# The z/u stage of a hybrid decoder layer: low parts one block later, sums and chain copies earlier, norms moved into v's stage, half of x first

## The chip, the cores and the metric

One core of a Trainium2 chip runs the whole program in one launch. The metric is the time of one execution on the device, in microseconds (us); the kernel before took 1266.7 us in the median of three runs (1266.69 to 1267.68). The engines in this text are PE (matmul), DVE (VectorE), ACT (ScalarE), POOL (GpSimd) and SP, which here only issues loads.

## The reference, cut to what matters

```python
h = x @ w_in[i]                         # x: 1024 tokens x 1024
u = gelu(h[..., 3*D_ATTN : 3*D_ATTN + D_GMLP])
z = gelu(h[..., 3*D_ATTN + D_GMLP :])
gm = _chunked_gmlp(u, z, ...)           # u * (W_s @ LN(z) + b)
mix = concat([attention(q, k, v), gm]) @ w_o
x = LN1(ALPHA * x + mix)                # then the convolved feed-forward, LN2,
x = LN3(ALPHA * x + gate * ple)         # and the gated input embedding
```

All data are float32. Only the first part, z, u and the v that follows, is touched by the change.

## The kernel before, in words

A float32 product is made of three matmuls with values that are split in a high and a low part (`mm3`, lines 131 to 134). `split` (line 115) makes them: ACT copies the source into a high part, DVE subtracts that from the source, which gives the low part. A matmul of 128x128 by 128x512 is the unit of work.

z and u are 1024 x 512 each, and h is made from x (both halves of its 1024 columns) by a Strassen scheme with seven products instead of eight. Tokens come in four pairs of 128 (`tp` or `j`), an "even" and an "odd" block in each pair. The even blocks with the first and the second half of x's columns are a11 and a12 of the scheme, the odd ones a21 and a22; the weights are the blocks "11", "21" (of z's columns) and "12", "22" (of u's), each in two pieces of 128 x 2 x 512. Product p takes four token blocks (`xop_of`) and one weight block (`wst[p, s]`, two pieces) and runs 48 matmuls: `zu_product` goes through the four k blocks of 128 columns and in each through the four j (product 0: j outside). Products 0, 3, 4 and 6 add into the PSUM chain X (`zbank`, the two tiles zA), product 1 into Y, products 2 and 5 into Z; Y and Z lie in the same four banks (B, B, D0, D1). `zu_evac` takes a chain's value out after a product: ACT copies it (p = 0, 2, 3; a Gelu for 6), DVE adds it to what lies in z or u (1, 4, 5). `s_sum` makes the sums S1 to S4 of x's blocks on DVE, in place where the raw x lies (S3 into half of a z page), `s_split` splits them, and `t_sum` makes the sums of the weights in place of the raw weights. The raw x of the first column half lies in the tile u.

The order is written by hand (`manual_schedule`): each engine runs its instructions in the order of the Python program, and waits by semaphores for the data and for buffers. Buffers come from pools: 12 weight pieces ("w"), 24 pages ("pg"), two raw buffers ("raw"), three large ones ("L"). SP issues loads in the program's order too, so a load that waits for a buffer holds back those behind it.

Then comes v (`dense_pair`, tile vps): it needs the even and odd blocks of x and the four pieces of a further weight (`Wv`). x's odd blocks of the first column half are loaded once more (256 KB each, into the raw buffers), since their place is u's by then. `z_norm` is a layer norm of one block of z and its split; two are done before v, six within it. v's first tiles are those of the chain X, so v waits for z's last copies (`zu_evac(6, j)`).

Of the kernel before, what the change touches and what calls it, by code (L numbers as in the profile page):

```python
# [51 lines left out]
def hybrid_layer(ctx, tc, x, xT, pT, pos, w_in, ln_z_g, ln_z_b, w_sT, b_sT, w_o,  # L52
# [134 lines left out]

    def put_x(kh, i, src):
        X[kh][i] = page([128, 2, 4, 128], F32R, "xhl")
        split(X[kh][i][:, 0], X[kh][i][:, 1], src)  # L190
# [59 lines left out]
    load_x(1, 3)  # L250
    SP.dma_start(ident, c_id)
# [15 lines left out]
    for k in range(1, 4):  # L267
        first_x(k)
# [64 lines left out]
    def s3raw(tp):  # L333
        return zp[tp][:, 1, :].rearrange("p (k c) -> p k c", c=128)

    def s_split(n, tp):
        if n > 2:
            d = sop[n + 1, tp] = page([128, 2, 4, 128], F32R, "zs")
            split(d[:, 0], d[:, 1], s3raw(tp) if n == 3 else raw_x(1, tp, 0))
# [4 lines left out]
        split(d[:, 0], d[:, 1], raw_x(0, tp, 2 - n))  # L344

    zu_product(0)
# [3 lines left out]
    split_wraw(1, "21", 1)  # L350
    zu_product(1)
    for s_ in range(2):
        load_wraw("12", s_)
    for s_ in range(2):
        load_wraw("22", s_)
# [5 lines left out]
    for s_ in range(2):  # L361
# [5 lines left out]
    zu_product(2)  # L367
    for tp in range(4):
        s_sum(2, tp)
        s_split(2, tp)  # L370
    def t_sum(dst, a, b, s_):
        DVE.tensor_tensor(wraw[dst, s_], wraw[a, s_], wraw[b, s_], OP.subtract)

    t_sum("11", "22", "11", 0)
    split_wraw(3, "11", 0)
    t_sum("11", "22", "11", 1)
    split_wraw(3, "11", 1)
    zu_product(3)
    for tp in range(4):
        s_sum(3, tp)  # L380
        s_split(3, tp)
    t_sum("12", "22", "12", 0)
    split_wraw(4, "12", 0)
    for tp in range(4):
        s_sum(4, tp)
    for j in range(4):
        zu_evac(3, j)
    t_sum("12", "22", "12", 1)
    split_wraw(4, "12", 1)
    for j in range(4):  # L390
        zu_evac(2, j)
        ACT.activation(zp[j][:, 0, :], zp[j][:, 0, :], AF.Gelu)
# [3 lines left out]
    split_wraw(5, "22", 0)  # L396
    split_wraw(5, "22", 1)
    for tp in range(4):
        put_x(1, 2 * tp + 1, raw_x(1, tp, 1))
    for s_ in range(2):  # L400
        t_sum("21", "21", "11", s_)
    for j in range(4):
        zu_evac(4, j)
    zu_product(5)
# [3 lines left out]
    for s_ in range(2):  # L408
        split_wraw(6, "21", s_)
    for j in range(4):  # L410
        ACT.activation(u[:, 2 * j + 1, :], u[:, 2 * j + 1, :], AF.Gelu)
    znh = big([128, NT, 512], F32R, "znh")
    znl = big([128, NT, 512], F32R, "znl")

    def z_norm(i):
        zz = zp[i // 2][:, i % 2, :]
        ln_dve(zz, zz, *ln_stats(zz, 512), gbz[:, 0, :], gbz[:, 1, :])
        split(znh[:, i, :], znl[:, i, :], zz)

    for j in range(4):  # L420
        zu_evac(5, j)
# [55 lines left out]
    for j in range(4):  # L477
        pa = psA("vps")
        g = dense_pair(j, W, pa)
        if j == 0:  # L480
            next(g)
            z_norm(1)
            next(g)
            z_norm(3)
        if j == 1:
            next(g)
            z_norm(4)
            next(g)
            z_norm(6)
        if j == 2:  # L490
            next(g)
            z_norm(5)
            next(g)
            z_norm(7)
# [768 lines left out]
    n = 0  # L1263
# [372 lines left out]
```

## Time and profile before

| | us |
|---|---|
| median of three runs | 1266.7 |
| profiled execution | 1266.69 |
| span of that execution (first to last instruction) | 1265.0 |
| PE busy | 1205.4 (95%) |
| DVE busy | 888.1 (70%) |
| ACT busy | 562.8 (44%) |
| first matmul of v | 121.75 |

The profiled execution lies 1.7 us above its span, at the fastest of the three runs. A timeline gives an instruction's start and length; in brackets stands the idle time of its engine before it, and what ended that. The length of a matmul is modelled and overlaps the next one's start, so its pace is read from one start to the next.

### The profile page before, as it was taken

To read this page: it belongs to the slowest core of one execution; us is meant where nothing else is said; L and a number is where in the kernel's file an instruction comes from. 1 tells how busy PE (TensorE), PEld (TensorE's weight loads), DVE (VectorE), ACT (ScalarE), POOL (GpSimd) and SP (SyncE) were. 2 spreads that over 40 slices of the span, in tenths; PEclk is the share of its full clock that TensorE was granted. 3 is DMA by queue.
4 is the path that set the end of the run, shared out by engine and by line. 5 is a ranking of instruction groups with operands and counts; after the bars stand their busy time and mean duration, and the time that the engine had idled before them with its cause. 6 is when DMAs were issued, how large, how long until landed. Compare 5 with 4: busy or idle time off the path is not lost. (4 is left out here: it accounts for less than half of the span.)

```text
span 1265.0 us, 15813 instructions
## 1 busy us (share of the span) xinstructions
PE 1205.4 (95%) x5788; PEld 1003.3 (79%) x5788; DVE 888.1 (70%) x1319; ACT 562.8 (44%) x972; POOL 467.9 (37%) x371
## 2 busy tenths in 40 slices
PE   8784999998999997999999999999999999999997
PEld 6673888887887886888888888888878888888886
DVE  4675653435788888576667776667776985798876
ACT  4263221437786672553443443444454344541221
POOL 0000100233342645666677766677710000022443
PEclk8897999999999999999999999999999999999999
DMA  7013254320020213203333213333379544640001
GB/s 285 0 34 104 80 200 167 117 67 18 1 84 34 84 59 127 67 2 124 125 125 125 87 47 117 125 125 125 96 263 340 194 128 130 217 164 26 34 34 50
DMA packets 64125, 136.93 MB, mean 108 GB/s; under 512 B 5552, under 2 KB 25392, under 8 KB 64048
## 3 DMA queue, kind: packets, MB, share of 16 engines
q1 hardware_dynamic: 62176, 129.51, 30.0%
q10 hardware_dynamic: 1872, 6.42, 1.3%
q8 instruction: 45, 0.74, 0.2%
q14 instruction: 32, 0.26, 0.1%
HBM read 101.05 MB, written 34.87 MB: 107 GB/s over the span
## 5 line engine op out<-in xcount | busy, mean ns | idle before, releaser
L166 POOL TENSOR_TENSOR rs<-rs,neg 128x1 f32<-128x1 f32 x24 | 21.1, 877 | 398.3 <-DVE rs L165 398.3
L132 PE MATMUL P<-xop,wop 128*128 128x512 f32 (+1 forms) x376 | 146.2, 389 | 0.0
L134 PE MATMUL P<-xop,wop 128*128 128x512 f32 (+1 forms) x376 | 145.3, 386 | 0.0
L133 PE MATMUL P<-xop,wop 128*128 128x512 f32 (+1 forms) x376 | 145.1, 386 | 0.0
L117 POOL TENSOR_TENSOR wop<-s,wop 128x512 fp32r<-128x512 f32 x62 | 94.2, 1525 | 86.4 <-ACT wop L111 86.4
L117 POOL TENSOR_TENSOR wop<-raw,wop 128x512 fp32r<-128x512 f32 x64 | 101.3, 1597 | 35.3 <-ACT wop L111 35.1
L111 ACT ACTIVATE aop<-raw 128x512 fp32r<-128x512 f32 x77 | 48.2, 626 | 92.1 <-DMA raw<-hid_d 65.2
L111 ACT ACTIVATE wop<-s 128x512 fp32r<-128x512 f32 x66 | 41.3, 626 | 99.8 <-DVE s L1163 53.4
L134 PEld LDWEIGHTS P<-xop,wop 128*128 128x128 f32 x376 | 71.2, 189 | 14.1
L132 PEld LDWEIGHTS P<-xop,wop 128*128 128x128 f32 x376 | 71.2, 189 | 13.9
L133 PEld LDWEIGHTS P<-xop,wop 128*128 128x128 f32 x376 | 71.2, 189 | 13.8
L117 DVE TENSOR_TENSOR aop<-raw,aop 128x512 fp32r<-128x512 f32 x77 | 56.8, 738 | 23.1 <-ACT aop L111 23.1
L1238 DVE SCALAR_TENSOR_TENSOR ht<-ct,mask,ht 128x1023 f32<-128x1023 f32 x22 | 47.9, 2176 | 31.4 <-ACT ht L1237 31.3
L133 PE MATMUL P<-bop,aop 128*128 128x512 f32 x176 | 68.8, 391 | 0.6 <-DVE bop L117 0.6
L132 PE MATMUL P<-bop,aop 128*128 128x512 f32 x176 | 68.6, 390 | 0.0
L134 PE MATMUL P<-bop,aop 128*128 128x512 f32 x176 | 68.5, 389 | 0.0
L111 ACT ACTIVATE wop<-raw 128x512 fp32r<-128x512 f32 x66 | 39.6, 626 | 61.6 <-DMA raw<-in_w_b_dram 39.0
L132 PE MATMUL D<-xop,wop 128*128 128x512 f32 (+1 forms) x176 | 66.9, 380 | 0.0
L134 PE MATMUL D<-xop,wop 128*128 128x512 f32 (+1 forms) x176 | 66.8, 379 | 0.0
L133 PE MATMUL D<-xop,wop 128*128 128x512 f32 (+1 forms) x176 | 66.8, 379 | 0.0
L1245 POOL TENSOR_TENSOR ht<-ht,ct 128x1024 f32<-128x1024 f32 x22 | 57.2, 2598 | 14.5 <-ACT ht L1242 14.5
L111 ACT ACTIVATE ct<-P 128x512 f32<-128x512 f32 x68 | 40.3, 593 | 45.4 <-PE P L134 42.8
(366 smaller groups left out, 3502.5 us busy)
## 6 DMA issues: line engine op xcount, KB each, us to landing
raw<-hid_d SPq DMA_DIRECT2D x35, 512.0 KB, 3.9
hid_d<-ct SPq DMA_DIRECT2D x22, 512.0 KB, 5.6
wd<-in_w_down_dram SPq DMA_DIRECT2D x44, 256.0 KB, 5.8
hid_d<-ht SPq DMA_DIRECT2D x33, 256.0 KB, 4.7
raw<-in_w_in_dram SPq DMA_DIRECT2D x12, 512.0 KB, 3.5
raw<-in_w_a_dram SPq DMA_DIRECT2D x11, 512.0 KB, 4.0
raw<-in_w_b_dram SPq DMA_DIRECT2D x11, 512.0 KB, 6.0
wraw<-in_w_a_dram SPq DMA_DIRECT2D x11, 512.0 KB, 5.5
```

The costliest lines, as they stand in the source:

```text
L111: ACT.activation(dst, src, AF.Copy)
L117: lo_eng.tensor_tensor(lo, src, hi.bitcast(F32), OP.subtract)
L132: PE.matmul(ps, sh, mh, start=first, stop=False, skip_group_check=chain)
L133: PE.matmul(ps, sh, ml, start=False, stop=False, skip_group_check=chain)
L134: PE.matmul(ps, sl, mh, start=False, stop=last, skip_group_check=chain)
L166: POOL.tensor_tensor(rs, rs, neghalf, OP.pow)
L1238: DVE.scalar_tensor_tensor(t[:, 1:S], c[:, 0:S - 1], cw[:, f, 1:2], t[:, 1:S], op0=OP.mult, op1=OP.add)
L1245: POOL.tensor_tensor(tt[g, e], tt[g, e], ctile[g, 1, e], OP.mult)
```

## The change

It has five parts.

- Low parts wait in a list (`lows`). `split_d` issues the high part on ACT at once and keeps DVE's subtraction back until the next block's high part has been issued; `flush` empties the list. Weight blocks are split, and their sums made, in halves of 128x512.
- `s_sum` runs one block ahead of its split; the S3 and S4 sums are made before the second weight piece of product 3, ahead of the splits that need a free page; the chain copies `evacs(p)` stand earlier, in front of the next weight sum, and the Gelu of z is no longer between chain 2's copies.
- Of the first column half of x, the even blocks are loaded first and the odd ones behind all of x's second half.
- SP's reloads for v alternate: two of x, two weights, two of x, two weights; the norm's vectors (`gbz`) come behind them, not ahead.
- The two z norms ahead of v move into v's first three pairs, and each norm's scaling stands behind the next one's statistics.

On DVE, from chain 1's adds to the sums for product 3 (L327 and L340 are S2's sums, L362, L372 and L361 weight sums, L117 and L196 low parts; zs and wil are the low parts' tiles, L342 and L344 the S3 and S4 sums). Before:

```order
L362 TENSOR_TENSOR wraw<-wraw 128x1024
L117 TENSOR_TENSOR wil<-wraw,wih 128x1024
L327 TENSOR_TENSOR u<-u 128x4x128
L117 TENSOR_TENSOR zs<-u,zs 128x512
L327 TENSOR_TENSOR u<-u 128x4x128
L117 TENSOR_TENSOR zs<-u,zs 128x512
L327 TENSOR_TENSOR u<-u 128x4x128
L117 TENSOR_TENSOR zs<-u,zs 128x512
L327 TENSOR_TENSOR u<-u 128x4x128
L117 TENSOR_TENSOR zs<-u,zs 128x512
L372 TENSOR_TENSOR wraw<-wraw 128x1024
L117 TENSOR_TENSOR wil<-wraw,wih 128x1024
```

Now:

```order
L196 TENSOR_TENSOR zs<-u,zs 128x512
L340 TENSOR_TENSOR u<-u 128x4x128
L196 TENSOR_TENSOR zs<-u,zs 128x512 x2
L361 TENSOR_TENSOR wraw<-wraw 128x512 x2
L196 TENSOR_TENSOR zs<-u,zs 128x512
L196 TENSOR_TENSOR wil<-wraw,wih 128x512 x2
L342 TENSOR_TENSOR z<-raw,u 128x512
L342 TENSOR_TENSOR z<-xraw,u 128x512 x3
L344 TENSOR_TENSOR raw<-raw,u 128x4x128
L344 TENSOR_TENSOR xraw<-xraw,u 128x4x128 x3
L361 TENSOR_TENSOR wraw<-wraw 128x512 x2
L196 TENSOR_TENSOR wil<-wraw,wih 128x512 x2
```

The low parts of S2 no longer alternate with its sums, a weight's sum and its low part have other work between them, and eight x sums stand ahead of the second weight piece.

On ACT, ahead of v (L429 and L457 are u's Gelu, L304 and L317 z's last copies, the wih are v's weights, znh the norms' high parts). Before:

```order
L111 ACTIVATE xhl<-raw 128x512 x4
L429 ACTIVATE u<-u 128x512 x4
L111 ACTIVATE wih<-raw 128x1024 x3
L111 ACTIVATE znh<-z 128x512 x2
L304 ACTIVATE z<-zA 128x512 x4
L111 ACTIVATE wih<-raw 128x1024
L111 ACTIVATE znh<-z 128x512 x2
```

Now:

```order
L111 ACTIVATE xhl<-raw 128x512 x2
L111 ACTIVATE wih<-raw 128x1024 x2
L111 ACTIVATE xhl<-raw 128x512 x2
L457 ACTIVATE u<-u 128x512 x4
L317 ACTIVATE z<-zA 128x512 x4
L111 ACTIVATE wih<-raw 128x1024 x2
L111 ACTIVATE znh<-z 128x512 x2
```

z's last copies now stand ahead of the third weight and of all norms, and behind the second pair of reloaded x.

On SP, from the last z/u weights to v (L425 and L445 are the reloads of x, gbz the norm's vectors). Before:

```order
L229 DMA wraw<-in_w_in_dram 128x1024 x4
L137 DMA gbz<-in_ln_z_g_dram 128x512
L137 DMA gbz<-in_ln_z_b_dram 128x512
L425 DMA raw<-in_xT_dram 128x4x128 x4
L125 DMA raw<-in_w_in_dram 128x1024 x4
L513 DMA raw<-in_w_sT_dram 128x1024
```

Now:

```order
L240 DMA wraw<-in_w_in_dram 128x1024 x4
L445 DMA raw<-in_xT_dram 128x4x128 x2
L125 DMA raw<-in_w_in_dram 128x1024 x2
L445 DMA raw<-in_xT_dram 128x4x128 x2
L125 DMA raw<-in_w_in_dram 128x1024 x2
L137 DMA gbz<-in_ln_z_g_dram 128x512
L137 DMA gbz<-in_ln_z_b_dram 128x512
L547 DMA raw<-in_w_sT_dram 128x1024
```

The norm's vectors moved behind v's loads, which alternate now.

The diff, cut to its core:

```diff
+    lows = []
+    def flush(keep=0):
+        while len(lows) > keep:
+            lows.pop(0)()
+    def split_d(hi, lo, src, keep=1):
+        copy(ACT, hi, src)
+        lows.append(lambda: DVE.tensor_tensor(lo, src, hi.bitcast(F32), OP.subtract))
+        flush(keep)
     def put_x(kh, i, src):
-        split(X[kh][i][:, 0], X[kh][i][:, 1], src)
+        split_d(X[kh][i][:, 0], X[kh][i][:, 1], src)
...
     def split_wraw(p, blk, s):
-        split(hi, lo, wraw[blk, s])
+        for k in range(2):
+            split_d(hi[:, k], lo[:, k], wraw[blk, s][:, k])
...
     SP.dma_start(r0[:, 0:1], w_in[4, 0][:, 0:1])
-    SP.dma_start(x0[:, 0:1], xT[0, 0, :, 0:1, :])
+    SP.dma_start(x0[:, 0:2, 0:128], xT[0, 0, :, 0:2, 0:128])
     SP.dma_start(r0[:, 1:2], w_in[4, 0][:, 1:2])
-    for k in range(1, 4):
-        SP.dma_start(x0[:, k:k + 1], xT[0, 0, :, k:k + 1, :])
+    SP.dma_start(x0[:, 2:4, 0:128], xT[0, 0, :, 2:4, 0:128])
     load_wraw("11", 1)
     for tp in range(1, 4):
-        load_x(0, tp)
+        stage_x(0, tp)
+        SP.dma_start(raw_x(0, tp, 0), xT[0, tp, :, :, 0:128])
...
     load_x(1, 3)
+    for tp in range(4):
+        SP.dma_start(raw_x(0, tp, 1), xT[0, tp, :, :, 128:256])
...
-    for j in range(4):
-        zu_evac(0, j)
+    evacs(0)
+    s_sum(1, 0)
     for tp in range(4):
-        s_sum(1, tp)
+        if tp < 3:
+            s_sum(1, tp + 1)
         s_split(1, tp)
-    for s_ in range(2):
-        DVE.tensor_tensor(wraw["11", s_], wraw["12", s_], wraw["11", s_], OP.subtract)
-        split_wraw(2, "11", s_)
-        if s_ == 0:
-            for j in range(4):
-                zu_evac(1, j)
+    t_sum("11", "12", "11", 0)
+    split_wraw(2, "11", 0)
+    flush()
+    evacs(1)
+    t_sum("11", "12", "11", 1)
+    split_wraw(2, "11", 1)
+    flush()
     zu_product(2)
...
     split_wraw(3, "11", 0)
+    flush()
+    for tp in range(4):
+        s_sum(3, tp)
+    for tp in range(4):
+        s_sum(4, tp)
     t_sum("11", "22", "11", 1)
     split_wraw(3, "11", 1)
+    flush()
     zu_product(3)
     for tp in range(4):
-        s_sum(3, tp)
         s_split(3, tp)
     t_sum("12", "22", "12", 0)
     split_wraw(4, "12", 0)
-    for tp in range(4):
-        s_sum(4, tp)
-    for j in range(4):
-        zu_evac(3, j)
+    flush()
+    evacs(3)
     t_sum("12", "22", "12", 1)
     split_wraw(4, "12", 1)
...
+    evacs(5)
+    zu_product(6)
+    def reload_x(tp):
+        r = rawpage([128, 4, 128])
+        SP.dma_start(r, xT[0, tp, :, :, 128:256])
+        put_x(0, 2 * tp + 1, r)
+    Wv = group(2)
+    reload_x(0)
+    reload_x(1)
+    flush()
+    Wv.load(2)
+    reload_x(2)
+    reload_x(3)
+    flush()
+    for j in range(4):
+        ACT.activation(u[:, 2 * j, :], u[:, 2 * j, :], AF.Gelu)
+    evacs(6)
+    Wv.load(2)
...
-    Wv.load(3)
-    z_norm(0)
-    z_norm(2)
-    for j in range(4):
-        zu_evac(6, j)
-    Wv.load(1)
...
+        if j < 3:
+            for i in ((0, 2, 1), (3, 4, 6), (5, 7))[j]:
+                next(g)
+                z_norm(i)
```

## Rows read from the trace of the kernel before

**Rows 1.** The page, part 1: busy time, share of the span, instructions.
```profile
span 1265.0 us, 15813 instructions
...
PE 1205.4 (95%) x5788; PEld 1003.3 (79%) x5788; DVE 888.1 (70%) x1319; ACT 562.8 (44%) x972; POOL 467.9 (37%) x371
```

**Rows 2.** Waits of PE, 0 to 240 us: total us, times, longest.
```profile
PE vps L132 <- ACT z L304: 16.4, 1, 16.4
PE zA L132 <- ACT wih L111: 7.5, 2, 4.4
PE zA L132 <- ACT u L111: 3.8, 1, 3.8
PE B L132 <- DVE z L308: 1.8, 1, 1.8
```

**Rows 3.** Timeline of PE: start us, length, line, operation, [idle before <- releaser].
```profile
11.11 0.80 PE L132 MATMUL zA<-wih,xhl 128*128 128x512 f32 x1 [3.10 <-ACT wih L111]
...
12.38 0.80 PE L133 MATMUL zA<-wil,xhl 128*128 128x512 f32 x1 [0.47 <-DVE wil L117]
...
17.60 0.40 PE L133 MATMUL zA<-wil,xhl 128*128 128x512 f32 x1
...
24.19 0.39 PE L132 MATMUL B<-wih,xhl 128*128 128x512 f32 x1
...
36.99 0.47 PE L132 MATMUL B<-wih,zs 128*128 128x512 f32 x1 [1.76 <-DVE z L308]
...
52.51 0.79 PE L132 MATMUL zA<-wih,zs 128*128 128x512 f32 x1 [4.36 <-ACT wih L111]
...
70.75 0.50 PE L132 MATMUL zA<-wih,zs 128*128 128x512 f32 x1 [3.85 <-ACT u L111]
...
121.75 0.79 PE L132 MATMUL vps<-wih,xhl 128*128 128x512 f32 x1 [16.44 <-ACT z L304]
```

**Rows 4.** Windows: length, busy PE, PEld, DVE, ACT, POOL; clock; DMA share, GB/s.
```profile
30.00:40.00 10.00, 8.24 (x37) 6.52 (x36) 7.87 (x10) 1.83 (x3) 0.00 (x0) 1.00 0.02 7
...
53.00:54.00 1.00, 0.53 (x2) 0.24 (x2) 1.00 (x2) 0.00 (x0) 0.00 (x0) 0.50 0.00 0
```

**Rows 5.** Timeline of DVE, 43 to 71 us, columns as in rows 3.
```profile
43.48 0.69 DVE L117 TENSOR_TENSOR zs<-u,zs 128x512 fp32r<-128x512 f32 x1 [0.70 <-ACT zs L111]
...
65.16 1.22 DVE L372 TENSOR_TENSOR wraw<-wraw 128x1024 f32<-128x1024 f32 x1
...
69.33 1.89 DVE L331 TENSOR_TENSOR xraw<-xraw,u 128x512 f32<-128x512 f32 x3
```

**Rows 6.** Timeline of ACT, 3 to 123 us, columns as in rows 3.
```profile
3.54 0.63 ACT L111 ACTIVATE wih<-wraw 128x512 fp32r<-128x512 f32 x1 [1.46 <-DMA wraw<-in_w_in_dram]
...
10.01 1.06 ACT L111 ACTIVATE wih<-wraw 128x1024 fp32r<-128x1024 f32 x1 [2.52 <-DMA wraw<-in_w_in_dram]
...
21.52 0.63 ACT L111 ACTIVATE xhl<-xraw 128x512 fp32r<-128x512 f32 x1 [0.62 <-DMA xraw<-in_xT_dram]
...
69.53 2.38 ACT L111 ACTIVATE u<-zA 128x512 f32<-128x512 f32 x4 [1.98 <-DVE raw L331]
...
101.14 2.18 ACT L429 ACTIVATE u<-u 128x512 f32<-128x512 f32 x4
...
120.64 2.04 ACT L304 ACTIVATE z<-zA 128x512 f32<-128x512 f32 x4
```

**Rows 7.** DMA per half us, 0 to 20; u's loads; L425, L125 landing.
```profile
GB/s 0 0 0 45 164 379 260 160 199 127 277 311 389 344 369 361 410 410 410 418 393 434 426 401 434 401 401 418 418 442 401 410 393 401 401 426 426 382 358 374
...
u<-in_xT_dram SPq DMA_DIRECT2D x3, 512.0 KB, 8.0
...
DMA to landing us min/median/max: 3.1/3.9/4.7
...
DMA to landing us min/median/max: 3.4/3.5/4.9
```

**Rows 8.** Windows of 25 us, columns as in rows 4.
```profile
600.00:625.00 25.00, 25.00 (x112) 20.70 (x111) 15.54 (x15) 12.41 (x21) 18.18 (x13) 1.00 0.45 158
```

More of the change, by code (lines that the diff above doesn't have):

```diff
@@ L266, in hybrid_layer @@
     first_w(1)
-    for k in range(1, 4):
-        first_x(k)
+    first_x(2)
     split_wraw(0, "11", 1)
@@ L338, in s_split @@
             d = sop[n + 1, tp] = page([128, 2, 4, 128], F32R, "zs")
-            split(d[:, 0], d[:, 1], s3raw(tp) if n == 3 else raw_x(1, tp, 0))
+            split_d(d[:, 0], d[:, 1], s3raw(tp) if n == 3 else raw_x(1, tp, 0))
             return
@@ L343, in s_split, with t_sum, evacs @@
         d = sop[n + 1][:, tp]
-        split(d[:, 0], d[:, 1], raw_x(0, tp, 2 - n))
+        split_d(d[:, 0], d[:, 1], raw_x(0, tp, 2 - n))
+    def t_sum(dst, a, b, s_):
+        for k in range(2):
+            DVE.tensor_tensor(wraw[dst, s_][:, k], wraw[a, s_][:, k], wraw[b, s_][:, k], OP.subtract)
+    def evacs(p):
+        for j in range(4):
+            zu_evac(p, j)
+    flush()
     zu_product(0)
@@ L350, in hybrid_layer @@
     split_wraw(1, "21", 1)
+    flush()
     zu_product(1)
-    for s_ in range(2):
-        load_wraw("12", s_)
-    for s_ in range(2):
-        load_wraw("22", s_)
-    for j in range(4):
-        zu_evac(0, j)
+    for blk in ("12", "22"):
+        for s_ in range(2):
+            load_wraw(blk, s_)
+    evacs(0)
+    s_sum(1, 0)
     for tp in range(4):
-        s_sum(1, tp)
+        if tp < 3:
+            s_sum(1, tp + 1)
         s_split(1, tp)
-    for s_ in range(2):
-        DVE.tensor_tensor(wraw["11", s_], wraw["12", s_], wraw["11", s_], OP.subtract)
-        split_wraw(2, "11", s_)
-        if s_ == 0:
-            for j in range(4):
-                zu_evac(1, j)
+    t_sum("11", "12", "11", 0)
[5 more added lines that the diff above has]
+    flush()
     zu_product(2)
+    s_sum(2, 0)
     for tp in range(4):
-        s_sum(2, tp)
+        if tp < 3:
+            s_sum(2, tp + 1)
         s_split(2, tp)
-    def t_sum(dst, a, b, s_):
-        DVE.tensor_tensor(wraw[dst, s_], wraw[a, s_], wraw[b, s_], OP.subtract)
     t_sum("11", "22", "11", 0)
     split_wraw(3, "11", 0)
+    flush()
[3 more added lines that the diff above has]
+        s_sum(4, tp)
     t_sum("11", "22", "11", 1)
     split_wraw(3, "11", 1)
+    flush()
     zu_product(3)
     for tp in range(4):
-        s_sum(3, tp)
         s_split(3, tp)
@@ L383, in hybrid_layer @@
     split_wraw(4, "12", 0)
-    for tp in range(4):
-        s_sum(4, tp)
-    for j in range(4):
-        zu_evac(3, j)
+    flush()
+    evacs(3)
     t_sum("12", "22", "12", 1)
     split_wraw(4, "12", 1)
-    for j in range(4):
-        zu_evac(2, j)
-        ACT.activation(zp[j][:, 0, :], zp[j][:, 0, :], AF.Gelu)
+    flush()
     zu_product(4)
@@ L396, in hybrid_layer @@
     split_wraw(5, "22", 0)
+    flush()
+    evacs(2)
+    for j in range(4):
+        ACT.activation(zp[j][:, 0, :], zp[j][:, 0, :], AF.Gelu)
+    for s_ in range(2):
+        t_sum("21", "21", "11", s_)
     split_wraw(5, "22", 1)
+    flush()
+    zu_product(5)
     for tp in range(4):
         put_x(1, 2 * tp + 1, raw_x(1, tp, 1))
[L400 to L404, printed above, removed]
-    gbz = page([128, 2, 512], F32, "gbz")
-    bcast(gbz[:, 0, :], ln_z_g, 512)
-    bcast(gbz[:, 1, :], ln_z_b, 512)
-    for s_ in range(2):
-        split_wraw(6, "21", s_)
+    flush()
+    evacs(4)
+    split_wraw(6, "21", 0)
+    flush()
     for j in range(4):
         ACT.activation(u[:, 2 * j + 1, :], u[:, 2 * j + 1, :], AF.Gelu)
[L412 to L421, printed above, removed]
+    split_wraw(6, "21", 1)
+    flush()
+    evacs(5)
     zu_product(6)
-    for tp in range(4):
+    def reload_x(tp):
         r = rawpage([128, 4, 128])
@@ L427, in hybrid_layer, with z_norm, z_last @@
     Wv = group(2)
+    reload_x(0)
+    reload_x(1)
+    flush()
+    Wv.load(2)
+    reload_x(2)
+    reload_x(3)
+    flush()
     for j in range(4):
         ACT.activation(u[:, 2 * j, :], u[:, 2 * j, :], AF.Gelu)
-    Wv.load(3)
-    z_norm(0)
-    z_norm(2)
-    for j in range(4):
-        zu_evac(6, j)
-    Wv.load(1)
-    W = Wv
+    evacs(6)
+    Wv.load(2)
+    W = Wv
+    gbz = page([128, 2, 512], F32, "gbz")
+    bcast(gbz[:, 0, :], ln_z_g, 512)
+    bcast(gbz[:, 1, :], ln_z_b, 512)
+    znh = big([128, NT, 512], F32R, "znh")
+    znl = big([128, NT, 512], F32R, "znl")
+    z_prev = []
+    def z_norm(i):
+        zz = zp[i // 2][:, i % 2, :]
+        stats = ln_stats(zz, 512)
+        z_last()
+        z_prev.append((i, zz, stats))
+    def z_last():
+        if z_prev:
+            i, zz, stats = z_prev.pop()
+            ln_dve(zz, zz, *stats, gbz[:, 0, :], gbz[:, 1, :])
+            split_d(znh[:, i, :], znl[:, i, :], zz)
     def dense_pair(j, W, pa):
@@ L479, in hybrid_layer @@
         g = dense_pair(j, W, pa)
[L480 to L494, printed above, removed]
+        if j < 3:
+            for i in ((0, 2, 1), (3, 4, 6), (5, 7))[j]:
+                next(g)
+                z_norm(i)
+            if j == 2:
+                z_last()
+                flush()
         if j == 3:
```

4 lines of the change are left out of this document (2 added, 2 removed).

## The prediction

> **What bounds the kernel now.** I read the page's busy table first: TensorE (PE) is busy 1205.4 of 1265.0 us [rows 1], so time can only come from stretches in which PE stands still or runs slowly. PE's own waits in the first 240 us list 16.4 us before the first matmul of v (vps), 7.5 us for two high parts of z/u weights, 3.8 us for a copy of a PSUM chain and 1.8 us for another [rows 2]. PE's order in time says where: before the second weight block (11.11, and again 0.47 us at 12.38), before products 2, 3 and 4 of the seven (36.99, 52.51, 70.75) and before v (121.75) [rows 3]. In that timeline the reader is to see the bracket, which is idle time and what ended it, and the steps between starts: 29 steps from 17.60 to 24.19 are 0.227 us each, the 12 from 12.38 to 17.60 take 5.22 us, 0.435 each. The granted clock says why: after the idle time before 52.51 it is 0.50 at 53 to 54 us, the lower level (1.2 GHz), while 30 to 40 us stands at 1.00, the upper one (2.4 GHz) [rows 4]. A wait thus costs itself and then about 0.2 us a matmul for a dozen matmuls.
>
> Last I read who is late at each place. On DVE and ACT the low part of a split follows its high part at once, so DVE stands 0.70 us for ACT at every block, as at 43.48, and a weight sum comes behind four such pairs, as at 65.16 [rows 5]. ACT's chain copies wait in turn, as at 69.53 [rows 6]. So z/u is bound by two engines that take turns, and v by a serial chain of loads, norms and copies.
>
> **The change, part by part.** The sum runs to the start of v, since PE has no wait worth naming from there to 240 us [rows 2] and is back to dense work then; v and all behind it should move as one.
>
> *Start.* The second weight block stands behind 768 KB instead of 1024 KB. Adding the half-microsecond slices, 1573 kB had moved at 7.67 us [rows 7], and the block, the last of those 1573, was taken at 10.01 [rows 6]: a lag of 2.3. The first weight had a lag of 0.6 (262 kB at 2.9, taken at 3.54). Now the block ends at 1311 kB, moved at 6.97 us; it lands at 7.6 with the small lag and 9.3 with the large. I take 8.6, nearer the large, since x loads still follow it, though half as big. Its halves are split apart now: 0.63 for the first high half [rows 6] and 0.69 for its low one [rows 5], so the matmul that stood at 12.38 stands at 8.6 + 0.63 + 0.69 + 0.12 for two hand-overs = 10.04. Gain 2.34 (1.6 to 3.3). The wait shrinks from 3.10 to about 1.4, below the 1.76 after which products went on at full step (36.99), so 12 slow steps go too: 5.22 - 12 x 0.227 = 2.5. Together 4.84; product 0 ends at 19.35 instead of 24.19.
>
> The Trainium skill ("DMA: Bandwidth & Descriptors", Queues, rings and completion order) has a DMA's semaphore land once every earlier write of that engine has landed, which makes only what is ahead count. By that the small lag would hold, and the sum would be 1.0 us larger; the row of 10.01, with its lag of 2.3, does not agree.
>
> Do the later loads still come in time? x's last second-half block was taken at 21.52 [rows 6]; it has 1024 KB less ahead now, some 2.5 us at the 410 GB/s of full slices [rows 7], so 19.0 to 19.6, and product 1 needs it at 19.35 + 9 x 0.227 = 21.4. The odd halves end 1 MB later, at about 22.6, mask and the first "12" weight 1 MB after that, at 25.2; four DVE/ACT passes make it 27.9, and product 2 needs it at 19.35 + 10.9 = 30.2. Hidden, with 1.8 and 2.3 us to spare; gone, each costs what it exceeds.
>
> *Products 1 to 2.* Both use the same PSUM banks, so product 2 waits for DVE's adds of chain 1, which stood behind a weight sum and its low part. That low part is now done at 27.9, and the first bank of product 1 only at 30.2 - 9 x 0.227 = 28.2; the adds run while product 1 ends, and the 1.76 goes.
>
> *Products 2 to 3.* Idle 4.36; then product 3 lasts 66.90 - 52.51 = 14.39 from start to the end of its last matmul, where 47 steps of 0.227 and a last length of 0.40 make 11.07 [rows 3]: 3.32 for the second wait and the slow clock. What is late next is DVE. From the end of product 1 it has the last chain add, then 2 weight sums, 2 lows, 4 x sums, 4 lows, 2 sums, 2 lows: 17 passes of 0.61 (three in a row take 1.89 [rows 5]) = 10.4, and product 3 starts 10.9 after that end: in time by half a microsecond. But eight x sums and a weight half are put ahead of its second weight block: 26 passes x 0.61 = 15.9, 0.4 for hand-overs and 0.63 for ACT give 16.9, where PE wants it at 10.9 + 5.45 = 16.35; the low half is another 0.5 late. I charge 1.1 (0 to 3). Gain 4.36 + 3.32 - 1.1 = 6.6.
>
> *Products 3 to 4.* Idle 3.85, and products 4 to 6 last until 121.75 - 16.44 = 105.31, which is 34.56, instead of 143 x 0.227 + 0.40 = 32.86: 1.7. The four S4 sums and the weight sum that held the chain copies back are done earlier; a first weight half late by 0.1 remains. Gain 5.4.
>
> *v.* PE waited for the first z copy at 120.64 [rows 6], which stood on ACT behind the high parts of two z norms; these norms go into v, which they enter after the last weight's low part (their gains and biases are loaded behind the weights, before that part is done). What is late next is the loads. Two raw buffers serve x's four odd halves and four weights in turn, and SP issues each when the low part of the one before it has been read. The second x half's low part now stands on DVE behind chain 5's adds, and it frees its buffer 2.2 us after product 6 starts (bank done 0.2, add 0.61, two lows). Everything SP has still to issue stands behind it. Then, in a row: weight load 4.2 (3.4 to 4.9 [rows 7]), high 1.06 and low 1.22, x load 3.5 (3.1 to 4.7, median 3.9 with other loads beside it), high 0.55, four Gelu 2.18, two of the four z copies 1.02 [rows 6], 0.2 for hand-overs: 16.1 after product 6 started, which lasts 10.9. The wait is 5.2 (4.0 to 7.1) instead of 16.44: gain 11.2. The slow clock behind it stays: even 3.85 of idle brought it [rows 3].
>
> *Small.* Weight blocks split in halves cost 0.1 us of ACT and 0.07 of DVE a block, inside the passes above. Each of four waits removed also gives back 0.16, since a matmul's modelled 0.40 overlaps the next's start by that much: 0.6.
>
> Sum: 4.84 + 1.76 + 6.6 + 5.4 + 11.2 + 0.6 = 30.4. The profiled execution took 1266.69 (span 1265.0 and 1.7 around it), the median is 1266.7, so the forecast is **1236.3**, with its own range from the bounds: +2 for the late stall, +2 and -1.2 for v's loads, +-0.85 at the start, 1233 to 1241.
>
> **The rivals.** *Loads crowd v.* If both trips in v's chain took 8.0 us, as x's loads do in the crowded start [rows 7], instead of 4.2 and 3.5, v would start 8.3 later: 1244.6. For it: eight loads follow each other on one queue. Against: only two are out at a time, as in the rows of 3.1 to 4.9. Chance 0.11.
>
> *DVE becomes the bound.* If passes hand over as badly as before in half a dozen places (0.70 each), product 3 starts 4 us late and a dozen matmuls run at the lower level, 2.5: 1242.8. Against: at least one independent pass stands between high and low now. Chance 0.07.
>
> *The clock, slower.* In products 1 to 6, a stage without pauses could be granted less. At the lower level each matmul costs 0.2 us more, so 152 of the stage's 336 at it would eat the 30.4, and all of them would give 1236.3 + 67 = 1303. Against: at 600 to 625 us PE is busy throughout, 112 matmuls, at 1.00 [rows 8]. The Trainium skill ("TensorE: Matmul & The Clock Gate", Part 1) says that the throttled state is the default and activity releases it; by that rule denser work can only help, and the trace agrees. Chance 0.03.
>
> *The change doesn't reach the end.* If a later stage paced by something else swallowed the gain, the time would stay at 1266. All later loads are issued against buffers that PE's own work frees, so I find no such pacer. Chance 0.02.
>
> **How the numbers follow.** Forecast 0.75, loads 0.11, DVE 0.07, clock 0.03, swallowed 0.02, and 0.02 for a still larger gain, below 1233. Range 1232 to 1242: it leaves out the worse half of the loads and of DVE's case, the clock, and the swallowed gain. Under 0.2% (2.5 us) nothing can be told from no change. Faster 0.95, same 0.02, slower 0.03.
>
> **What would show it.** Right: PE goes from product 0 to the end of 6 with no wait over 1.5 us; the granted clock stays at 1.00 from 10 to 80 us; v starts near 91 after a wait of about 5 us put down to a z copy; products 2 and 3 start at 30 and 41. Wrong: a wait over 3 us inside the products (DVE), the third and fourth weight of v landing after 95 (loads), 1.2 GHz in a dense stretch (clock), or v early and the k stage at its old time (swallowed).

## The result and the profile after

The changed kernel takes 1235.76 us in the median (1235.5 to 1236.74, four runs); the kernel before took 1267.19 beside it (1266.69 to 1268.31). The ratio is 0.9752, 95% interval 0.9735 to 0.9769. The forecast was 1236.3, range 1232 to 1242. The profiled execution of the changed kernel took 1236.74 us, with a span of 1235.0, 30.0 less than the span of before [rows 1]. In two of the experiments below one execution lies far off (4259.94 and 1833.71 us), and their medians are those of the other three.

The page, part 1, busy time of the engines:

```profile
span 1235.0 us, 15846 instructions
...
PE 1198.8 (97%) x5788; PEld 999.3 (81%) x5788; DVE 887.2 (72%) x1338; ACT 561.9 (46%) x983; POOL 467.8 (38%) x371
```

The work is the same to 1 us on DVE, ACT and POOL. PE is busy 6.6 us less for the same 5788 matmuls, and the other 23.4 us were idle time. PE's waits from 0 to 240 us (total, times, longest) answer to [rows 2]:

```profile
PE vps L132 <- ACT z L317: 4.6, 1, 4.6
PE zA L132 <- ACT wih L111: 2.2, 2, 1.7
...
PE zA L133 <- DVE wil L196: 0.2, 1, 0.2
```

The timeline of PE answers to [rows 3]:

```profile
9.14 0.71 PE L132 MATMUL zA<-wih,xhl 128*128 128x512 f32 x1 [1.68 <-ACT wih L111]
9.87 0.79 PE L133 MATMUL zA<-wil,xhl 128*128 128x512 f32 x1
...
20.57 0.39 PE L132 MATMUL B<-wih,xhl 128*128 128x512 f32 x1
...
31.45 0.39 PE L132 MATMUL B<-wih,zs 128*128 128x512 f32 x1
...
42.34 0.39 PE L132 MATMUL zA<-wih,zs 128*128 128x512 f32 x1
...
48.44 0.50 PE L132 MATMUL zA<-wih,zs 128*128 128x512 f32 x1 [0.50 <-ACT wih L111]
49.17 0.50 PE L133 MATMUL zA<-wil,zs 128*128 128x512 f32 x1 [0.22 <-DVE wil L196]
...
54.59 0.50 PE L132 MATMUL zA<-wih,zs 128*128 128x512 f32 x1
...
92.24 0.79 PE L132 MATMUL vps<-wih,xhl 128*128 128x512 f32 x1 [4.64 <-ACT z L317]
```

Products 1, 2, 3 and 4 start at 20.57, 31.45, 42.34 and 54.59 and follow each other without a gap that has a releaser. The two waits inside product 3 and the one ahead of v are all that is left from product 1 on. By stages, from the starts here and in [rows 3]:

| stage | before, us | after, us | gain | predicted |
|---|---|---|---|---|
| to the start of product 1 | 24.19 | 20.57 | 3.62 | 4.84 |
| product 1, to the start of 2 | 12.80 | 10.88 | 1.92 | 1.92 |
| products 2 and 3, to the start of 4 | 33.76 | 23.14 | 10.62 | 10.77 |
| products 4 to 6, to the start of v | 51.00 | 37.65 | 13.35 | 12.91 |
| sum, to the start of v | 121.75 | 92.24 | 29.51 | 30.44 |

The prediction's terms are laid on these stages with its 0.16 for each removed wait, and its 5.4 for "products 3 to 4" split into 3.85 ahead of product 4 and 1.55 behind it. The last 0.5 us of the 30.0 came behind v's start, so nothing there took the gain back. It is the difference of two larger amounts that go with the clock: the stretch behind a wait of 1.19 us takes 6.36 us now (277.86 to 284.22) and took 7.80 before (306.98 to 314.78), 1.44 less; and the 10 us behind a wait of 3.80 run at a granted clock of 0.71 (from 474.54) instead of 0.83 (before, from 505.10), and by 908.04 (before, 937.63) 0.97 is lost again.

The windows (length, busy time and count of PE, PEld, DVE, ACT, POOL; granted clock; DMA share, GB/s) answer to [rows 4]:

```profile
10.00:13.00 3.00, 3.00 (x8) 2.37 (x9) 2.31 (x4) 1.99 (x5) 0.00 (x0) 0.55 1.03 406
...
30.00:40.00 10.00, 10.00 (x46) 8.29 (x45) 9.84 (x17) 3.71 (x7) 0.00 (x0) 1.00 0.00 0
...
92.00:98.00 6.00, 5.76 (x14) 4.50 (x15) 3.49 (x6) 3.17 (x5) 0.00 (x0) 0.50 0.71 231
```

DVE is now busy 9.84 of 10 us beside a full PE, where it had 7.87 in [rows 4]: it is the engine that comes next in this stage. Up to 240 us the clock fell to the lower level (1.2 GHz, 0.50) at two places, behind the first wait and behind v's start.

ACT's timeline ahead of v answers to [rows 6]:

```profile
8.46 1.15 ACT L111 ACTIVATE wih<-wraw 128x512 fp32r<-128x512 f32 x2 [0.90 <-DMA wraw<-in_w_in_dram]
...
81.65 1.06 ACT L111 ACTIVATE wih<-raw 128x1024 fp32r<-128x1024 f32 x1 [6.75 <-DMA raw<-in_w_in_dram]
...
87.12 0.63 ACT L111 ACTIVATE xhl<-raw 128x512 fp32r<-128x512 f32 x1 [3.10 <-DMA raw<-in_xT_dram]
88.51 0.63 ACT L111 ACTIVATE xhl<-raw 128x512 fp32r<-128x512 f32 x1 [0.76 <-DMA raw<-in_xT_dram]
89.05 2.17 ACT L457 ACTIVATE u<-u 128x512 f32<-128x512 f32 x4
91.13 2.03 ACT L317 ACTIVATE z<-zA 128x512 f32<-128x512 f32 x4
```

The second weight block of product 0 was taken at 8.46. Ahead of v stands the chain that the prediction named: SP issues two weights at 78.08, ACT takes the first at 81.65, two reloads of x follow, the second of which ACT takes at 88.51, then four Gelu and z's copies, and PE starts after the second copy.

### The profile page after: what moved, and what is told of

The parts are those of the page before. It is cut to its first block, busy times and chain, and to the rows that moved or that the text cites. A ratio compares the mean times of both kernels' runs of the same rounds, so it can differ in the third digit from the quotient of the medians.

```text
span 1235.0 us, 15846 instructions
## 1 busy us (share of the span) xinstructions
PE 1198.8 (97%) x5788; PEld 999.3 (81%) x5788; DVE 887.2 (72%) x1338; ACT 561.9 (46%) x983; POOL 467.8 (38%) x371
## 5 line engine op out<-in xcount | busy, mean ns | idle before, releaser
L117 POOL TENSOR_TENSOR wop<-s,wop 128x512 fp32r<-128x512 f32 x62 | 94.1, 1524 | 86.1 <-ACT wop L111 85.8
L117 POOL TENSOR_TENSOR wop<-raw,wop 128x512 fp32r<-128x512 f32 x64 | 101.2, 1598 | 36.2 <-ACT wop L111 36.1
L117 DVE TENSOR_TENSOR aop<-raw,aop 128x512 fp32r<-128x512 f32 x77 | 54.7, 710 | 22.8 <-ACT aop L111 22.6
```

## The experiments

Each edit is made on the changed kernel, and its time stands beside that kernel's 1235.76, the median of executions that spread over 1.24 us. Beside the time I compare starts in the trace: product 1 at 20.57, product 4 at 54.59, v at 92.24. From product 1's start to v's start the changed kernel takes 71.67 us. This stretch is the better measure of an edit to it, since it holds neither what the clock does at the kernel's start nor what it does behind v's start. Both differ from one execution to the next, as shown below.

**Whole x blocks in the old order of loads.**

```diff
-    SP.dma_start(x0[:, 0:2, 0:128], xT[0, 0, :, 0:2, 0:128])
+    SP.dma_start(x0[:, 0:2], xT[0, 0, :, 0:2])
...
-        stage_x(0, tp)
-        SP.dma_start(raw_x(0, tp, 0), xT[0, tp, :, :, 0:128])
+        load_x(0, tp)
...
-    for tp in range(4):
-        SP.dma_start(raw_x(0, tp, 1), xT[0, tp, :, :, 128:256])
```

> The changed kernel with the loads of x in the old order (both halves of each pair together, ahead of the second column half). My theory: the second weight block lands 1.5 us later again (10.0 instead of 8.46), the halves of the block keep their share, and the lower clock lasts some 1 us longer, so 2 to 3 us over the changed kernel's 1235.8, about 1238.3; the later products keep their pace. Rival: the whole start term (3.6 us between the two traces) belongs to the loads: 1239.4 or more. Other rival: the odd halves, which now come early, make up for it: 1236.

Measured: 1237.65, the median of three (ratio 0.9753 to 0.9785). The time came near the expected 1238.3, but not by its mechanism. ACT's timeline shows that the second weight block came no later with 1024 KB ahead of it:

```profile
8.40 1.15 ACT L111 ACTIVATE wih<-wraw 128x512 fp32r<-128x512 f32 x2 [1.13 <-DMA wraw<-in_w_in_dram]
```

How much the landing of one block varies is read from the nine kernels with the changed kernel's loads, whose SP issues it at 2.69 or 2.70 in each. ACT took it between 7.76 and 8.67; two of them, both edits undone (below) and the last experiment:

```profile
7.90 1.15 ACT L111 ACTIVATE wih<-wraw 128x512 fp32r<-128x512 f32 x2 [1.58 <-DMA wraw<-in_w_in_dram]
```

```profile
8.67 1.15 ACT L111 ACTIVATE wih<-wraw 128x512 fp32r<-128x512 f32 x2 [0.93 <-DMA wraw<-in_w_in_dram]
```

So 8.40 is no different from them. That doesn't make it a clean test of bytes, since the halves also move in smaller packets: in the first 5 us 414 of the changed kernel's 737 packets have 512 bytes to 2 KB, none of the 470 here.

From product 1 to v this kernel takes 73.56 us, 1.89 more. PE's timeline shows it, in product 3 and in the wait ahead of v (0.26 more is ahead of product 2):

```profile
48.30 0.50 PE L132 MATMUL zA<-wih,zs 128*128 128x512 f32 x1 [1.14 <-ACT wih L111]
...
92.81 0.80 PE L132 MATMUL vps<-wih,xhl 128*128 128x512 f32 x1 [5.38 <-ACT z L314]
```

So loading one half of x first is not what brings the weight early. It helps DVE later: the last block of x's second column half is taken at 18.87 in the changed kernel and at 20.03 here, and DVE is less behind in products 2 and 3. The 0.74 more ahead of v is a load's: ACT takes the second of v's weights 2.15 us behind the first here and 1.31 behind it in the changed kernel, which the edit doesn't explain.

**Four loads or six ahead of the second weight.** The rival cause is the number of loads: before, six were issued ahead of that block, now four. Here the halves stay, in six loads.

```diff
-    SP.dma_start(x0[:, 0:2, 0:128], xT[0, 0, :, 0:2, 0:128])
+    SP.dma_start(x0[:, 0:1, 0:128], xT[0, 0, :, 0:1, 0:128])
     SP.dma_start(r0[:, 1:2], w_in[4, 0][:, 1:2])
-    SP.dma_start(x0[:, 2:4, 0:128], xT[0, 0, :, 2:4, 0:128])
+    for k in range(1, 4):
+        SP.dma_start(x0[:, k:k + 1, 0:128], xT[0, 0, :, k:k + 1, 0:128])
```

> The changed kernel with the first even block of x loaded in four pieces of 64 KB again, as many loads as before, but only its even half (768 KB in all ahead of the second weight block, as in the changed kernel). Theory one (the number of loads ahead counts, not their bytes): the second weight block is issued at about 3.6 us instead of 2.69 and taken by ACT at 9.2 to 10.0 instead of 8.46, so its wait grows by 0.7 to 1.5 us and the time is 1236 to 1238. Rival (bytes count, and the like arrival with whole halves had another reason): taken at 8.2 to 8.7, time 1235 to 1236.5.

Measured: 1236.11 (ratio 0.9744 to 0.9771). SP's and ACT's timelines:

```profile
3.61 0.43 SPq L240 DMA_DIRECT2D wraw<-in_w_in_dram  x1
...
9.66 1.15 ACT L111 ACTIVATE wih<-wraw 128x512 fp32r<-128x512 f32 x2 [1.77 <-DMA wraw<-in_w_in_dram]
```

Theory one holds for the arrival: with the same 768 KB ahead, the block is issued 0.92 us later than in the changed kernel (2.69) and taken at 9.66, 1.0 us behind the latest of the nine with four loads. From issue to ACT those nine have 5.07 to 5.98 us, whole blocks 5.74, six loads 6.05 and, before, 10.01 - 3.60 = 6.41 (six loads, 1024 KB). Of the 1.55 us that separate before from after, 0.9 is thus the issue, about 0.46 for each load of SP. The other 0.6 is smaller than the 0.9 by which the nine differ among themselves, and how it divides between loads and bytes is not shown. The profiled execution (1236.62) hardly differs from the changed kernel's (1236.74): here the clock held (below), product 1 starts at 20.49, and a wait of 2.32 us at the full clock cost about as much as 1.68 behind which it fell.

**Low parts at once.**

```diff
-        flush(keep)
+        flush()
```

> The changed kernel with every low part at once behind its high part (nothing kept back), all else as changed. Theory one (either cover will do): the sums that run one block ahead already stand between a high part and its low part, so only the waits at weights grow: 1 to 2.5 us over the changed kernel, 1237 to 1238.3. Theory two (the low parts' delay carries products 2 to 4): the 0.70 us a block come back in ten or so blocks, 5 to 8 us, 1241 to 1244.

Measured: 1239.07 (1235.97 to 1240.21; ratio 0.9757 to 0.9792), 3.3 more, between the two theories. In the trace, product 1 to v takes 72.58 us, only 0.91 more. PE's waits grow in two places there, product 3 and the start of product 4:

```profile
49.30 0.50 PE L132 MATMUL zA<-wih,zs 128*128 128x512 f32 x1 [1.15 <-ACT wih L111]
...
55.93 0.50 PE L132 MATMUL zA<-wih,zs 128*128 128x512 f32 x1 [0.35 <-ACT u L111]
```

Another 1.60 us is lost far behind v: the stretch behind the wait of 1.19 us, 6.36 in the changed kernel, takes 7.96 (279.08 to 287.04) at a granted clock of 0.79. So the trace speaks for theory one: of the 2.5 us by which this execution is longer, 0.9 is the edit's and 1.6 the clock's.

**Sums next to their splits.**

```diff
-    s_sum(1, 0)
     for tp in range(4):
-        if tp < 3:
-            s_sum(1, tp + 1)
+        s_sum(1, tp)
         s_split(1, tp)
...
-    for tp in range(4):
-        s_sum(3, tp)
-    for tp in range(4):
-        s_sum(4, tp)
     t_sum("11", "22", "11", 1)
...
     for tp in range(4):
+        s_sum(3, tp)
         s_split(3, tp)
...
+    for tp in range(4):
+        s_sum(4, tp)
     evacs(3)
```

S2 is edited like S1.

> The changed kernel with the sums of x in their old places (each ahead of its own split, S3 and S4 behind product 3's weights, S4 ahead of chain 3's copies), low parts still one block late. Theory one (either cover will do): the 1 us stall inside product 3 goes and up to 1.7 us comes at the start of product 4: within 1 us of the changed kernel, 1235 to 1236.8. Theory two (the places of the sums carry the gain): 5 to 8 us over it, 1241 to 1244.

Measured: 1237.63, the median of three (ratio 0.9751 to 0.9784), 1.9 more and 0.8 above theory one. Product 1 to v takes 71.49 us, 0.18 less, so the 1.9 is not lost there; the stretch behind the wait of 1.19 takes 7.85 again (276.56 to 284.41). The stall in product 3 is gone, as the prediction's account of it asks, and a wait for a chain copy stands ahead of product 4 instead:

```profile
PE zA L132 <- ACT u L111: 1.1, 1, 1.1
```

**Both undone.** The two edits above together.

> Both undone: low parts at once and sums in their old places; weight halves, copies, loads and norms as changed. Theory one (either cover will do): now the old hand-overs are back and most of the gain of products 1 to 4 is lost, 10 to 13 us over the changed kernel, 1246 to 1249, with waits at the starts of products 2, 3 and 4 and the lower clock behind the longer ones. Rival (each part has its own share, they add up): the sum of the two single results; if those are small, small again, under 1239.

Measured: 1248.57 (ratio 0.9838 to 0.9867), 12.8 more than the changed kernel, where the two alone cost 3.3 and 1.9. Product 1 to v takes 83.70 us, 12.0 more, where the two alone cost 0.9 and -0.2. PE's waits to 240 us, and DVE's from 20 to 62 us:

```profile
PE zA L132 <- ACT u L111: 4.9, 1, 4.9
...
PE B L132 <- DVE z L321: 2.7, 1, 2.7
PE zA L132 <- ACT wih L111: 1.9, 2, 1.1
```

```profile
DVE zs L196 <- ACT zs L111: 8.7, 12, 1.0
```

Those are the waits of 0.70 us of [rows 5]: twelve with both edits, one of 0.4 with either edit alone, and none for zs in the changed kernel. Any one independent pass between a high part and its low part hides the hand-over, and each of the two changes supplies one such cover. Their shares can't be added: each alone looks nearly worthless, and together they are worth 12.8.

**Two norms back ahead of z's last copies.**

```diff
-    evacs(6)
-    Wv.load(2)
     W = Wv
...
+    z_norm(0)
+    z_norm(2)
+    z_last()
+    flush()
+    evacs(6)
+    Wv.load(2)
+
...
-            for i in ((0, 2, 1), (3, 4, 6), (5, 7))[j]:
+            for i in ((1, 3), (4, 6), (5, 7))[j]:
```

> The changed kernel with two z norms (blocks 0 and 2) back ahead of z's last copies and of the third and fourth weight of v. My theory: v's first copies then wait for two norms, which take some 4.5 us longer than the loads do, so v starts 4 to 5 us later; in v nothing is won back: 4 to 5 us over the changed kernel, 1240 to 1241. Rival: the loads bound the start of v anyway, the norms hide behind them, under 1 us.

Measured: 1241.18 (ratio 0.9781 to 0.9814), 5.4 more; product 1 to v takes 75.94 us, 4.3 more. PE's and ACT's timelines show the norms' high parts (znh) ahead of the copies, and v's wait at 8.98 instead of 4.64:

```profile
91.39 0.63 ACT L111 ACTIVATE znh<-z 128x512 fp32r<-128x512 f32 x1 [2.19 <-DVE z L171]
92.91 0.63 ACT L111 ACTIVATE znh<-z 128x512 fp32r<-128x512 f32 x1 [0.89 <-DVE z L171]
93.45 2.04 ACT L317 ACTIVATE z<-zA 128x512 f32<-128x512 f32 x4
```

```profile
94.56 0.79 PE L132 MATMUL vps<-wih,xhl 128*128 128x512 f32 x1 [8.98 <-ACT z L317]
```

The norms are thus worth 4.3 of the 11.8 us that v's wait lost. (Their vectors are loaded ahead of the third and fourth weight here, and no wait ahead of v is put down to them.)

**Reloads without the alternation.** Four reloads of x, then four weights.

```diff
     reload_x(1)
-    flush()
-    Wv.load(2)
     reload_x(2)
...
     evacs(6)
-    Wv.load(2)
+    Wv.load(4)
```

> The changed kernel with v's reloads in straight order: the four odd blocks of x, then z's last copies, then the four weights. Theory one (the chain of two raw buffers is what v waits for, and the copies stand behind its last x block): the x blocks now come in the first two steps of the chain, the copies are done before the first weight, and v starts about 10.5 us after product 6 starts, with hardly a wait, but short waits for the second and third weight; 2 to 5 us under the changed kernel, 1231 to 1234. Theory two (the alternation is what made v's wait short): the weights come a whole step later and v waits 6 us or more; 2 to 4 us over it, 1238 to 1240.

Measured: 1232.78 (1231.76 to 1236.25; ratio 0.9715 to 0.9749), 3.0 less than the changed kernel, though one of the four executions is no faster. Product 1 to v takes 69.02 us, 2.65 less. PE's timeline:

```profile
87.88 0.50 PE L132 MATMUL vps<-wih,xhl 128*128 128x512 f32 x1 [2.12 <-ACT wih L111]
89.14 0.51 PE L133 MATMUL vps<-wil,xhl 128*128 128x512 f32 x1 [0.76 <-DVE wil L117]
```

ACT's timeline, the first two of z's copies:

```profile
84.44 1.09 ACT L317 ACTIVATE z<-zA 128x512 f32<-128x512 f32 x2 [1.50 <-PE zA L134]
```

Of the parts undone here the alternation is the one that costs: with it two trips to memory, weights and then x, stand in a row ahead of the copies. Without it z's copies wait only for PE, and v waits for its first weight, whose high part ACT makes behind those copies (at 86.77).

**Reloads early.** The first two reloads and their split go ahead of u's Gelu, chain 5's adds and product 6, so that their low parts no longer wait behind those adds.

```diff
     evacs(4)
     split_wraw(6, "21", 0)
+    flush()
+    reload_x(0)
+    reload_x(1)
     flush()
     for j in range(4):
...
     evacs(5)
     zu_product(6)
...
-    reload_x(0)
-    reload_x(1)
-    flush()
     Wv.load(2)
```

The definitions of `reload_x` and `Wv` move up with them.

> The changed kernel with the reload and split of x's first two odd blocks ahead of chain 5's adds and of product 6 (the loads stay alternating). My theory: those two low parts held the raw buffers until chain 5 was added; now the weights of v are asked for some 3.5 us earlier, v's wait falls from 4.6 to 1 to 1.5 us and the lower clock behind it goes or shortens: 3.5 to 6 us under the changed kernel, 1230 to 1232.5. Rival: another step sets v's wait (the copies on ACT behind the Gelu, or the landing of loads that now collide with product 6's reads), and it stays above 3.5: within 1 us.

Measured: 1229.72 (1229.33 to 1230.78; ratio 0.969 to 0.9719), 6.0 less than the changed kernel and the best of all runs. SP's, ACT's and PE's timelines and the window behind v's start:

```profile
72.28 0.94 SPq L125 DMA_DIRECT2D raw<-in_w_in_dram  x2
...
85.44 2.03 ACT L317 ACTIVATE z<-zA 128x512 f32<-128x512 f32 x4
```

```profile
86.55 0.50 PE L132 MATMUL vps<-wih,xhl 128*128 128x512 f32 x1 [0.66 <-ACT z L317]
```

```profile
92.00:98.00 6.00, 6.00 (x28) 4.97 (x27) 5.63 (x13) 1.27 (x2) 3.73 (x4) 1.00 0.35 119
```

Weights are issued at 72.28 instead of 78.08, the whole chain moves with them, and v's wait falls from 4.64 to 0.66. That is 4.0, as is product 1 to v (67.69 us). The rest goes with the clock, which stays at 1.00 behind v's start: 28 matmuls in the window where the changed kernel ran 14, and 34.13 us instead of 36.84 from v's start to PE's next matmul into a tile B. This execution also kept the full clock at its start (product 1 at 18.86), 1.71 us that the edit doesn't explain. The step of the prediction that the first low parts stand behind chain 5's adds, and that everything SP has still to issue stands behind them, is confirmed by this.

**Work for the first wait.** Six matmuls on zeros, into a bank that is not in use yet, fill PE's wait for the second weight block.

```diff
+                    if j == 0 and k == 2:
+                        for _ in range(6):
+                            PE.matmul(zt[1][:, 512:1024], warm[:, 0:128], warm, start=True, stop=True)
                     zu_mm(p, k // 2, k % 2, j)
```

> The changed kernel with six matmuls on zeros in a bank not yet in use, in PE's wait for the second weight block (about 1.4 us of work in a wait of 1.7). They change no result. My theory: it is the thin work of the first 9 us that lowers the clock there; with the wait filled the clock stays at 1.00 and nine slow matmuls go: 1 to 2 us under the changed kernel where its clock falls, about 1234.3. Rival: the clock falls all the same or the dummies delay the real matmuls: 1236 or more.

Measured: 1235.7 (1234.8 to 1236.99; ratio 0.9737 to 0.9766). In the profiled execution the clock from 10 to 13 us is 1.00 and v starts at 90.07, 2.2 earlier; the median is the same, between theory and rival. A reason that fits is in the other traces. The same window of three of them:

```profile
10.00:13.00 3.00, 3.00 (x15) 2.46 (x14) 2.32 (x5) 2.13 (x4) 0.00 (x0) 1.00 1.03 412
```

(early reloads; idle 1.23 at 8.73)

```profile
10.00:13.00 3.00, 2.43 (x9) 1.80 (x10) 2.65 (x5) 2.60 (x5) 0.00 (x0) 1.00 1.01 393
```

(six loads; idle 2.32 at 10.34)

```profile
10.00:13.00 3.00, 3.00 (x9) 2.32 (x8) 2.33 (x5) 2.12 (x4) 0.00 (x0) 0.51 1.04 409
```

(sums next to splits; idle 0.63 at 8.90)

Of the nine traces without the zeros, the clock fell here in three (the changed kernel, low parts at once, sums next to splits) and held in six. Where it held and the loads are as in the changed kernel, product 1 starts at 18.62 to 18.86 instead of 20.57. Zeros can gain only in executions in which it falls. The changed kernel's other three executions took 1235.5 to 1235.91 against the 1236.74 of the profiled one, at mean granted clocks of 0.992 and 0.993 against 0.990. That would fit a clock that held here in them; they have no trace, so where it held stays open.

**Together.** Early reloads, the zeros, and S4's sums behind the second weight piece of product 3.

```diff
-    for tp in range(4):
-        s_sum(4, tp)
     t_sum("11", "22", "11", 1)
     split_wraw(3, "11", 1)
     flush()
+    for tp in range(4):
+        s_sum(4, tp)
     zu_product(3)
```

> The kernel with early reloads (1229.7), and in addition six matmuls on zeros in the first wait of product 0 and the S4 sums behind the second weight piece of product 3. Theory one: the stall of 0.5 + 0.2 us inside product 3 goes, and the clock at the start never falls, which is worth up to 1.5 us in those executions in which it falls otherwise: 1228.0 to 1229.5. Rival: as with the zeros alone, the median does not move, and the later S4 sums hold back chain 2's copies: 1229.5 to 1231.

Measured: 1231.43 (1231.28 to 1233.62; ratio 0.9711 to 0.9738), 1.7 more than the early reloads alone: the rival's side, 0.4 above its range. PE's waits:

```profile
PE vps L132 <- ACT z L317: 1.6, 1, 1.6
...
PE zA L132 <- ACT u L111: 1.1, 1, 1.1
```

The stall of 0.50 and 0.22 in product 3 is gone, and 1.09 us ahead of product 4 has come for it. ACT's timeline shows the next weight's high parts, which stand ahead of that chain's copies, at 51.20:

```profile
51.20 1.15 ACT L111 ACTIVATE wih<-wraw 128x512 fp32r<-128x512 f32 x2 [3.70 <-DVE wraw L364]
52.26 2.04 ACT L111 ACTIVATE u<-zA 128x512 f32<-128x512 f32 x4
```

They wait for a weight sum on DVE and come 9.96 us behind product 3's start (41.24). With the early reloads alone they come at 50.58, also 9.96 behind that start (40.62), since DVE's passes up to that sum are the same and only their order differs. What has changed is that product 3 ends 1.35 us sooner, and PE meets the copies that it used to find done. With DVE busy 9.84 of 10 us a moved pass moves the wait: from product 1 to the start of product 5 PE gains 0.17 us. So the late S4 sums are not where the 1.7 was lost. In this trace v's wait is 1.55 instead of 0.66, because the last of x's four reloads, issued with the third at 78.36 (78.28 with the early reloads alone), is taken at 84.15 instead of 82.82, and the stretch behind the wait of 1.19 takes 7.88 us instead of 6.38.

The runs side by side (the early reloads are in the last one too):

| run | median, us | product 1 starts | product 1 to v |
|---|---|---|---|
| changed kernel | 1235.76 | 20.57 | 71.67 |
| whole x blocks | 1237.65 | 19.25 | 73.56 |
| six loads | 1236.11 | 20.49 | 71.79 |
| low parts at once | 1239.07 | 20.79 | 72.58 |
| sums next to splits | 1237.63 | 20.65 | 71.49 |
| both undone | 1248.57 | 18.74 | 83.70 |
| two norms back | 1241.18 | 18.62 | 75.94 |
| no alternation | 1232.78 | 18.86 | 69.02 |
| reloads early | 1229.72 | 18.86 | 67.69 |
| zeros | 1235.70 | 18.58 | 71.49 |
| together | 1231.43 | 19.48 | 68.40 |

Product 1 to v took 97.56 us before, so the change gained 25.9 there. Late low parts and early sums (12.0 if both are undone), the two norms (4.3), the order of x's loads (1.9) and the alternation (-2.6) account for 15.5 of it, if they are added. The weight halves, the earlier chain copies and the later norm vectors were not undone; that the other 10.4 is theirs is argued from the waits and not shown.

## Why the prediction was right, point by point

*Start: the arrival right in size, its reason not shown and the clock wrong.* The block was forecast at 8.6 and came at 8.46. The step "stands behind 768 KB instead of 1024 KB" put all of this down to bytes, and fails against 8.40 with 1024 KB and 9.66 with 768 KB: the change also cut the first block of x from four loads to two, and 0.9 of the 1.55 us is the time in which SP issues them. The first low half, forecast for 10.04, was there at 9.87. The second step that fails is "the wait shrinks ... below the 1.76 after which products went on at full step, so 12 slow steps go too". In the changed kernel's profile the clock did fall after 1.68: from 9.14 to 12.59 seven steps take 3.45 us, 0.42 to 0.73 each. The kernels with the same start in which it held begin product 1 at 18.62 to 18.86, 1.7 to 1.95 earlier, and the predicted 19.35 lies between the two cases; the 1.22 that the term is short of is less than this slow clock cost. Of the signs named, "no wait over 1.5 us" and a clock of 1.00 from 10 us on fail here. With the same instructions up to there it fell after 0.63 and held after 1.23, and with six loads it held after 2.32: no length of the pause decided it here.

The rule that was weighed at this term (the Trainium skill, "DMA: Bandwidth & Descriptors", Queues, rings and completion order) has a load's semaphore land once the earlier writes have landed. The traces agree that later loads did not hold the block, since more was queued behind it with whole x blocks (512 KB loads) and it came at 8.40, within the range of the others. The small lag of 0.6 that I drew from the rule was not there all the same: 1311 kB had moved by 6.9 us, and the block was taken 1.6 later.

*The later loads: right.* x's last second-half block, forecast for 19.0 to 19.6, was taken at 18.87, and no wait of PE is put down to it.

*Product 1 to 2: right.* DVE now waits 0.96 us for PE at chain 1's adds (29.61), instead of PE for DVE; 1.92 against 1.76 + 0.16.

*Products 2 and 3: right.* The new stall inside product 3 was put at 1.1 with bounds of 0 and 3; it is 0.50 + 0.22, and product 3 lasts 12.25 us from start to start where 48 steps make 10.90, so 1.35 by the same measure. With the sums in their old place it disappears, which shows that the eight sums ahead of the weight piece are its cause.

*Products 3 to 4: right.* No idle time has a releaser at 54.59.

*v: right, and a little better.* The wait is 4.64 for 5.2; v starts at 92.24 for 91.3, and the 1.22 of the start more than make up that difference. The weight trip took 3.57 us instead of 4.2 and the x trip 3.12 instead of 3.5, but the second block of x came 1.39 behind the first, which has no term in the sum. The loads did not crowd: the rival of 8.0 us a trip is out. The slow clock behind v's start, which the prediction kept, is there (0.50 from 92 to 98 us).

*The other rivals.* DVE as the bound needs hand-overs of 0.70; with both covers undone they come back twelve times and the time is 1248.6, so it was the right rival with the right price per pass, and one independent pass is what keeps it out. Dense work ran at 1.00 (30 to 40 us), against the slower clock. Behind v's start 0.5 us more was gained, against the gain swallowed.

*Luck.* The mechanism held from product 1 on, but that the total came within about half a microsecond of the forecast is in part luck. The start fell 1.22 short, products 2 to 6 gave 0.29 more, and the 0.5 behind v is what two moves of the clock left over. With the clock held at the start, as in four traces with the same loads, it would have been 1.7 to 1.95 us less.

*What the prediction would have shown had it looked further.* It took the alternation of v's reloads as given. Its own sum of that chain held two trips, and the other order has one: 3 us were to be had there, and 6 with the first reloads ahead of chain 5's adds. The two were not tried together.

## What to carry to other kernels

Where two engines hand a value over in every step, one independent pass between the two halves of the step hides the hand-over, wherever it comes from; undo such covers together before judging one of them. Count the trips to memory that stand in a row ahead of a stage, and start the first of them before the last engine that frees its buffer gets busy with something else. Early in a program put a wanted block behind few loads: each one ahead of it cost 0.46 us of issue here. And when an edit is worth 2 us or less, compare the stretch that it changes, not the total: a clock that falls in one execution and holds in the next moves the total as much.

## What the runs showed of the hardware that was not expected

- Each load ahead of the second weight block delayed its issue by about 0.46 us (3.61 behind six, 2.69 behind four). Once issued it took 5.07 to 5.98 us to be used in nine traces with the same loads, so that a landing seen in one trace is known to about 0.5 us either way; 5.74 with 1024 KB ahead lies within that.
- The granted clock behind PE's first wait falls or holds from one execution to the next with the same instructions up to there: it fell after idle times of 0.63 and 1.68 us and held after 0.55, 0.77 and 1.23. One profile can thus be 1.7 to 2 us off at its start, about the 1.9 us by which two of the experiments differ from the changed kernel.
- The same happens at 270 to 307 us, behind a wait of 1.18 or 1.19 us that stands in all twelve traces. In three of the twelve traces (the changed kernel, six loads, early reloads) the clock is 1.00 there and the stretch takes 6.36 to 6.38 us; in the other nine it is 0.78 to 0.80, and the stretch takes 7.77 to 7.96 us.
